# Conditioning and first norm: x loaded first, sums of squares, norm and splits in another order and in wider passes

## The chip, the cores and the metric

The kernel runs on one core of a Trainium2 chip. Its engines, as the profile names them: PE (TensorE, matrix products; PEld is its loading of the stationary operand), DVE (VectorE), ACT (ScalarE), POOL (GpSimd) and SP (SyncE, which here issues the DMAs). The metric is the device time of one execution in microseconds (us), as the median of several runs.

## The reference, cut to what matters

One layer of a hybrid diffusion backbone: 1024 latent tokens and 256 context tokens of width 1024. What the changed part computes is the conditioning, the first norm, the modulation and the operands of the input projection:

```python
sh1, sc1, ... = split(silu(c) @ w_ada + b_ada, 6)         # for the latents
cmods         = split(silu(c_ctx) @ w_ada + b_ada, 6)     # for the context
rmsnorm(x, g) = x * rsqrt(mean(x * x, axis=-1) + EPS) * g
h  = rmsnorm(x,   norm1_g) * (1 + sc1) + sh1
hc = rmsnorm(ctx, norm1_g) * (1 + cmods[1]) + cmods[0]
u  = h @ w_in                                             # 9280 columns
uc = hc @ w_in[:, :SSD_IN_WIDTH]
```

After it come a state-space scan, a Fourier branch, gates, an output projection and a feed-forward part; they are not touched.

## The kernel before

Activations lie transposed: channels on the 128 partitions, tokens along the free dimension. x is 8 tiles `xt[k]` of 128 x 1024, the context one tile `ct` of 128 x 8 x 256; k counts blocks of 128 channels. Products are taken in three passes: each operand is split into a rounded part (hi) and the rest (lo), and hi*hi + hi*lo + lo*hi is summed (`mm3m`, L210). So every normalised tile has to be cast (hi, on ACT) and subtracted (lo) before a product can use it, and so has every weight tile (`wsplit`, L198 and L199: hi on ACT, lo on GpSimd).

The first stage (L243 to L377) has these parts:

- *Conditioning.* `ada_k(hf, k)` (L259 to L265) multiplies the two vectors silu(c), silu(c_ctx) by one 512 KB weight tile `wa`: two matmuls of 2 x 512, which the profile shows as four records. hf = 0 gives shift and scale of the channel blocks 0 to 3, hf = 1 of 4 to 7. `ada_end(hf)` copies the result (`gr`, ACT), turns it onto partitions (`gtr`, 8 transposes) and makes `ada` and `sc1` of it on DVE. Five `wa` buffers are in turn.
- *Norm.* `sumsq` squares the 8 tiles on ACT and adds them on DVE; `rstd` sums the partitions with matmuls against a column of ones (`cps`, L287), adds EPS on DVE and takes the power -0.5 on GpSimd (L291); `rstd_bcast` makes diagonal blocks on DVE (L298) and spreads them over the partitions by a matmul (`bc`, L300, into PSUM).
- *Modulation.* For k < 4, x is multiplied by the broadcast (`normed`, L323, in halves of 512), scaled and shifted (L328), cast (L329), subtracted (L330). For k >= 4 the multiply takes the scale with it (L334), the cast the shift (L335). The context is multiplied by its broadcast (L352, eight instructions of 256), scaled and shifted on ACT (L338), cast on ACT (L339) and subtracted on GpSimd (L340), each per k.
- *First product.* `in_k` sums u's first 128 columns, for 512 + 512 latent and 256 context tokens, over k; what follows (the dt columns, the gate columns, pairs of blocks with sums of operands) runs on.

Inside this stage the order on PE and SP is the order in which the code is written (`manual_schedule`, L343). The order on DVE, ACT and GpSimd is laid out by a scheduler when the program is built; at run time it is fixed. Outside the stage the scheduler orders PE too, so products of the dt columns may lie between those of the first product. SP issues loads in the written order; `wraw` has two buffers, whi and wlo three.

In the written order before the change, the context's squares and column sums come first, x's after them, then x's broadcasts, `ada_k(1, 0)`, `ada_end(0)`, the modulation of k < 4, the other `ada_k(1, k)` and the first product.

Of the kernel before, what the change touches and what calls it, by code (L numbers as in the profile page):

```python
# [15 lines left out]
P = 128  # L16
D = 1024
KT = D // P
# [123 lines left out]
def _build(nc, tc, h, o, hook, stop, es):  # L142
# [86 lines left out]
    hc_hi = [hcpool.tile([P, LC], F32R, name=f"hchi{k}") for k in range(KT)]  # L229
    hc_lo = [hcpool.tile([P, LC], F32R, name=f"hclo{k}") for k in range(KT)]  # L230
# [13 lines left out]
    with pool("p0", "right") as p0, pool("pp0", "left", space=PSUM) as pp0:  # L244
# [22 lines left out]
        ada_load(0, 0)  # L267
        nc.sync.dma_start(out=ct, in_=h["cT"])
        ada_load(0, 1)
        for k in range(KT):  # L270
            nc.sync.dma_start(out=xt[k], in_=h["xT"][k])
            if k % 2 and k < 6:
                ada_load(0, 2 + k // 2)

        def sumsq(src, n, name):
            acc = p0.tile([P, n], F32, name=name)
            for k in range(KT):
                sq = acc if k == 0 else p0.tile([P, L], F32, name="sq", bufs=2)[:, :n]
                nc.scalar.activation(out=sq, in_=src(k), func=AF.Square)
                if k:  # L280
                    nc.vector.tensor_tensor(out=acc, in0=acc, in1=sq, op=ALU.add)
            return acc

        def rstd(sqacc, nt):
            cps = pp0.tile([P, 512], F32, name="cps", tag="cps", bufs=1)
            for t in range(nt):
                nc.tensor.matmul(cps[:, t:t + 1], lhsT=sqacc[:, t * P:(t + 1) * P], rhs=onec, start=True, stop=True)  # L287
# [37 lines left out]
        def modulated(k):  # L325
            sc, sh = sc1[:, 0, k:k + 1], ada[:, k, 0:1]
            if k < 4:
                nc.vector.tensor_scalar(out=xt[k], in0=xt[k], scalar1=sc, scalar2=sh, op0=ALU.mult, op1=ALU.add)  # L328
                nc.scalar.copy(out=h_hi[k], in_=xt[k])  # L329
                nc.vector.tensor_tensor(out=h_lo[k], in0=xt[k], in1=h_hi[k].bitcast(F32), op=ALU.subtract)  # L330
            else:
                for hf in range(2):
                    sl = slice(512 * hf, 512 * hf + 512)
                    nc.vector.scalar_tensor_tensor(out=xt[k][:, sl], in0=xt[k][:, sl], scalar=sc, in1=bcs[hf], op0=ALU.mult, op1=ALU.mult)  # L334
                nc.scalar.activation(out=h_hi[k], in_=xt[k], func=AF.Identity, bias=sh)  # L335
                nc.vector.scalar_tensor_tensor(out=h_lo[k], in0=xt[k], scalar=sh, in1=h_hi[k].bitcast(F32), op0=ALU.add, op1=ALU.subtract)
            cm = ct[:, k, :]
            nc.scalar.activation(out=cm, in_=cm, func=AF.Identity, scale=sc1[:, 1, k:k + 1], bias=ada[:, k, 1:2])  # L338
            nc.scalar.copy(out=hc_hi[k], in_=cm)  # L339
            nc.gpsimd.tensor_tensor(out=hc_lo[k], in0=cm, in1=hc_hi[k].bitcast(F32), op=ALU.subtract)  # L340

        gv = [[pp0.tile([P, 512], F32, name="gv", bufs=2) for _ in range(2)] for _ in range(2)]
        with tc.manual_schedule(engines={mybir.EngineType.PE, mybir.EngineType.SP}):  # L343
            ada_k(0, 0)
            csq = sumsq(lambda k: ct[:, k, :], LC, "csq")
            rsc = rstd(csq, 2)
            ada_k(0, 1)
            ada_k(0, 2)
            bcc = rstd_bcast(rsc, 0, 2)
            sqacc = sumsq(lambda k: xt[k], L, "sqacc")  # L350
            for k in range(KT):
                nc.vector.tensor_tensor(out=ct[:, k, :], in0=ct[:, k, :], in1=bcc[:, :LC], op=ALU.mult)  # L352
            for k in range(3, 6):
                ada_k(0, k)
            rs = rstd(sqacc, NT)
            for k in range(6, 8):
                ada_k(0, k)
            bcs = [rstd_bcast(rs, t0, 4) for t0 in (0, 4)]
            for k in range(4):
# [3 lines left out]
            ada_k(1, 1)  # L363
            for k in range(4):
                modulated(k)
            for k in range(2, 5):
                ada_k(1, k)
# [1333 lines left out]
```

## Time and profile before

| | |
|---|---|
| median of 3 runs | 2252.82 us (2246.53 to 2255.43) |
| profiled execution | 2255.23 us, span 2253.5 us |
| PE busy | 2164.4 us, 96% of the span |
| PEld busy | 1809.4 us, 80% |
| DVE busy | 1629.2 us, 72% |
| ACT busy | 991.6 us, 44% |
| POOL busy | 742.0 us, 33% |
| granted PE clock, mean | 0.987 |

The profile is of one execution. PE is busy nearly all the time; the busy share of its first fortieth of the span (56 us) is 7 tenths, as that of the last; of the others 8 or 9. A row of the timeline gives start, duration, engine, line, operation, output and inputs, how many instructions it merges, and in brackets how long the engine was idle ahead of it and what released it.

### The profile page before, as it was taken

Reading aid. Unit: us, or ns where it says so; the run is one execution under the profiler, and the core shown is the slowest. Engines: PE = TensorE matmul, PEld = TensorE weight load, DVE = VectorE, ACT = ScalarE, POOL = GpSimd, SP = SyncE. Lnnn points to the kernel's source line nnn. Section 1 sums busy time; section 2 is a strip of 40 time slices with the busy share of each in tenths; the row PEclk is TensorE's granted clock in tenths of the full one; section 3 lists DMA queues with packets and bytes.
Section 4 is the critical chain, followed back from the end, with each engine's and each line's share of the span. In section 5 each row is a group of like instructions: output and inputs, shape, how many; then the busy total and the mean of one; then the engine's idle time right before and its main releaser. Section 6 shows DMA issues by size and latency. Waiting matters only on the chain. (4 is left out here: it accounts for less than half of the span.)

```text
span 2253.5 us, 32731 instructions
## 1 busy us (share of the span) xinstructions
PE 2164.4 (96%) x11560; PEld 1809.4 (80%) x11560; DVE 1629.2 (72%) x2783; ACT 991.6 (44%) x2082; POOL 742.0 (33%) x610
## 2 busy tenths in 40 slices
PE   7999999999999999999999999998898999999997
PEld 1778888877889999999889887786676888887876
DVE  5888888997757777777636558826987567675578
ACT  4445444545345676676733212124422332334443
POOL 1532211010236455555521132144333333332222
PEclk8999999999999999999999999999899999999999
DMA  7222223333455455555454547541476234457765
GB/s 281 76 71 84 85 85 122 133 130 108 144 165 172 157 164 179 165 169 175 151 202 161 183 152 264 188 159 63 155 270 229 85 114 155 152 190 240 234 203 181
DMA packets 167101, 360.28 MB, mean 160 GB/s; under 512 B 17548, under 2 KB 57228, under 8 KB 166296
## 3 DMA queue, kind: packets, MB, share of 16 engines
q1 hardware_dynamic: 166936, 358.18, 47.7%
q8 instruction: 91, 1.49, 0.3%
q14 instruction: 74, 0.61, 0.1%
HBM read 267.34 MB, written 90.78 MB: 159 GB/s over the span
## 5 line engine op out<-in xcount | busy, mean ns | idle before, releaser
L199 POOL TENSOR_TENSOR wlo<-wraw,whi 128x1024 fp32r<-128x1024 f32 (+1 forms) x83 | 203.0, 2449 | 614.4 <-ACT whi L198 566.8
L203 PE MATMUL fill<-whi,hhi 128*128 128x256 f32 x768 | 222.4, 291 | 0.0
L198 ACT CAST whi<-wraw 128x1024 fp32r<-128x1024 f32 (+1 forms) x123 | 126.5, 1034 | 215.7 <-PE dm L210 82.9
L433 DVE SCALAR_TENSOR_TENSOR cv<-pad,vecs,cv 128x1282 f32<-128x1282 f32 (+1 forms) x128 | 211.0, 1678 | 9.1 <-ACT cv L430 8.7
L204 PE MATMUL fill<-wlo,hhi 128*128 128x256 f32 x768 | 215.8, 281 | 0.6 <-POOL wlo L199 0.6
L205 PE MATMUL fill<-whi,hlo 128*128 128x256 f32 x768 | 216.0, 282 | 0.0
L915 ACT ACTIVATE abc<-abc,a_all 128x128 f32<-128x128 f32 x512 | 157.8, 390 | 96.2 <-DMA abc<-s_a 93.4
L203 PE MATMUL fp<-m,oph 128*128 128x512 f32 x452 | 180.3, 400 | 12.5 <-ACT oph L1384 10.5
L205 PE MATMUL fp<-m,opl 128*128 128x512 f32 x452 | 180.4, 400 | 9.6 <-DVE opl L1385 6.7
L204 PE MATMUL fp<-m,oph 128*128 128x512 f32 x452 | 180.2, 399 | 0.0
L496 PE MATMUL mm<-tq,whi 128*128 128x512 f32 x480 | 153.9, 401 | 2.3 <-ACT whi L198 2.3
L203 PEld LDWEIGHTS fill<-whi,hhi 128*128 128x128 f32 x768 | 144.1, 188 | 2.2 <-ACT ust L807 0.4
L204 PEld LDWEIGHTS fill<-wlo,hhi 128*128 128x128 f32 x768 | 144.6, 188 | 1.6 <-POOL wlo L199 0.8
L205 PEld LDWEIGHTS fill<-whi,hlo 128*128 128x128 f32 x768 | 144.3, 188 | 0.5
L496 PE MATMUL mm<-hhi,whi 128*128 128x512 f32 x320 | 128.2, 402 | 3.4 <-DVE pad L572 3.4
L496 PE MATMUL mm<-hlo,whi 128*128 128x512 f32 x320 | 127.6, 399 | 0.0
L496 PE MATMUL mm<-hhi,wlo 128*128 128x512 f32 x320 | 127.6, 400 | 0.0
L203 PEld LDWEIGHTS fp<-m,oph 128*128 128x128 f32 x452 | 85.9, 190 | 34.2 <-ACT oph L1384 11.7
L205 PEld LDWEIGHTS fp<-m,opl 128*128 128x128 f32 x452 | 85.6, 189 | 33.8 <-DVE opl L1385 9.7
L917 DVE COPY_PREDICATED abc<-misc,abc 128x512 f32<-128x512 int32 x64 | 50.8, 793 | 85.0 <-ACT abc L915 84.8
L496 PEld LDWEIGHTS mm<-tq,whi 128*128 128x128 f32 x480 | 89.7, 189 | 23.7 <-ACT whi L198 3.4
L891 DVE SCALAR_TENSOR_TENSOR S<-S,ead,st 128x64 f32<-128x64 f32 x512 | 104.7, 271 | 0.0
(411 smaller groups left out, 5929.4 us busy)
## 6 DMA issues: line engine op xcount, KB each, us to landing
abc<-s_a SPq DMA_DIRECT2D x64, 512.0 KB
fraw<-in_wfi SPq DMA_DIRECT2D x44, 512.0 KB
wraw<-in_wxbc SPq DMA_DIRECT2D x32, 512.0 KB
dx<-in_wada SPq DMA_DIRECT2D x32, 512.0 KB
wraw<-in_wzf SPq DMA_DIRECT2D x24, 512.0 KB
gt<-s_gate SPq DMA_DIRECT2D x24, 512.0 KB
fi<-in_wfo SPq DMA_DIRECT2D x22, 512.0 KB
s_cw<-fo SPq DMA_DIRECT2D x44, 256.0 KB
```

The costliest lines, as they stand in the source:

```text
L198: nc.scalar.copy(out=hi[:, :cols], in_=raw[:, :cols])
L199: (eng or nc.gpsimd).tensor_tensor(out=lo[:, :cols], in0=raw[:, :cols], in1=hi[:, :cols].bitcast(F32), op=ALU.subtract)
L203: nc.tensor.matmul(ps, lhsT=a[0], rhs=b[0], start=start, stop=False)
L204: nc.tensor.matmul(ps, lhsT=a[0], rhs=b[1], start=False, stop=False)
L205: nc.tensor.matmul(ps, lhsT=a[1], rhs=b[0], start=False, stop=stop)
L433: nc.vector.scalar_tensor_tensor(out=v[:, :n], in0=pd[:, t:t + n], scalar=cwh[:, 5 * b + t:5 * b + t + 1], in1=v[:, :n], op0=ALU.mult, op1 ...
L496: nc.tensor.matmul(ps, lhsT=lhs[x], rhs=b[i][y], start=i == 0 and (x, y) == (0, 0), stop=i == 3 and (x, y) == (1, 0))
L891: nc.vector.scalar_tensor_tensor(out=sn[:, hd_], in0=S[-1][:, hd_], scalar=decp[:, i, d, 4 * g + j:4 * g + j + 1], in1=sv_[:, hd_], op0=AL ...
L915: nc.scalar.activation(out=abc[:, d, j, :], in_=abc[:, d, j, :], func=AF.Identity, scale=-1.0, bias=a_all[:, c, hd:hd + 1])
L917: nc.vector.copy_predicated(out=E, mask=tri_b.bitcast(mybir.dt.int32)[:, None, :].to_broadcast([P, HPG, P]), data=abc[:, 1])
```

## The change

All of it lies in the first stage.

- SP loads x and the first four `wa` tiles in turn, then the fifth `wa`, the context, the first projection weights, the dt weights and the next five `wa`. The loads of the gate weights and of two later projection tiles stand ahead of the last of the `wa`.
- x's squares, column sums and broadcasts come before the context's. The context is squared in two passes of 1024 and added in one (`ctx_squares`); its column sums take four matmuls per 128 tokens, where one was enough. They stand behind x's broadcasts on PE, its broadcast behind `ada_k(1, 1)`.
- The context's multiply is one instruction of 2048.
- Modulation is the same for all k: `normed` for all eight, then cast with scale and shift on ACT (L338), scale and shift in place on DVE (L339), subtraction on DVE (L340). The context's cast and subtraction take four k at once, the subtraction on DVE (L348). The first weight tile's lo is taken on DVE.
- `in_k` of k = 0 to 3 stands before `ada_end(1)`, where only k = 0 did.

```diff
--- before.py
+++ after.py
@@ -226,8 +226,8 @@
     nc.sync.dma_start(out=rows, in_=h["rows"].broadcast_to([P, 160]))
     phA = ExitStack()
     hcpool = phA.enter_context(pool("hcpool", "right"))
-    hc_hi = [hcpool.tile([P, LC], F32R, name=f"hchi{k}") for k in range(KT)]
-    hc_lo = [hcpool.tile([P, LC], F32R, name=f"hclo{k}") for k in range(KT)]
+    hch2, hcl2 = [[hcpool.tile([P, 4, LC], F32R, name=f"{nm}{hf}") for hf in range(2)] for nm in ("hchi", "hclo")]
+    hc_hi, hc_lo = [[t[k // 4][:, k % 4, :] for k in range(KT)] for t in (hch2, hcl2)]
 
     ppm = phA.enter_context(pool("ppm", "left", space=PSUM))
 
@@ -264,27 +264,38 @@
             for s in range(2):
                 nc.tensor.matmul(gv[hf][s][:2, :], lhsT=sv[:, :, k], rhs=w[:, s, :], start=(k == 0), stop=(k == KT - 1))
 
-        ada_load(0, 0)
-        nc.sync.dma_start(out=ct, in_=h["cT"])
-        ada_load(0, 1)
         for k in range(KT):
             nc.sync.dma_start(out=xt[k], in_=h["xT"][k])
-            if k % 2 and k < 6:
-                ada_load(0, 2 + k // 2)
-
-        def sumsq(src, n, name):
-            acc = p0.tile([P, n], F32, name=name)
+            if k % 2 == 0:
+                ada_load(0, k // 2)
+        ada_load(0, 4)
+        nc.sync.dma_start(out=ct, in_=h["cT"])
+
+        def sq_tile():
+            return p0.tile([P, L], F32, name="sq", bufs=2)
+
+        def x_squares():
+            acc = p0.tile([P, L], F32, name="sqacc")
             for k in range(KT):
-                sq = acc if k == 0 else p0.tile([P, L], F32, name="sq", bufs=2)[:, :n]
-                nc.scalar.activation(out=sq, in_=src(k), func=AF.Square)
+                sq = sq_tile() if k else acc
+                nc.scalar.activation(out=sq, in_=xt[k], func=AF.Square)
                 if k:
                     nc.vector.tensor_tensor(out=acc, in0=acc, in1=sq, op=ALU.add)
-            return acc
-
-        def rstd(sqacc, nt):
+            return lambda t: [acc[:, t * P:t * P + P]]
+
+        def ctx_squares():
+            c = [sq_tile() for _ in range(2)]
+            for hf in range(2):
+                nc.scalar.activation(out=c[hf], in_=ct[:, 4 * hf:4 * hf + 4, :].rearrange("p a b -> p (a b)"), func=AF.Square)
+            nc.vector.tensor_tensor(out=c[0], in0=c[0], in1=c[1], op=ALU.add)
+            return lambda t: [c[0][:, q * LC + t * P:q * LC + t * P + P] for q in range(4)]
+
+        def rstd(parts, nt):
             cps = pp0.tile([P, 512], F32, name="cps", tag="cps", bufs=1)
             for t in range(nt):
-                nc.tensor.matmul(cps[:, t:t + 1], lhsT=sqacc[:, t * P:(t + 1) * P], rhs=onec, start=True, stop=True)
+                ps = parts(t)
+                for q, a_ in enumerate(ps):
+                    nc.tensor.matmul(cps[:, t:t + 1], lhsT=a_, rhs=onec, start=q == 0, stop=q == len(ps) - 1)
             ms = p0.tile([P, 16], F32, name="ms", bufs=2)
             nc.vector.tensor_scalar(out=ms[:, :nt], in0=cps[:, :nt], scalar1=EPS, scalar2=None, op0=ALU.add)
             rs = p0.tile([P, 16], F32, name="rs", bufs=2)
@@ -324,56 +335,54 @@
 
         def modulated(k):
             sc, sh = sc1[:, 0, k:k + 1], ada[:, k, 0:1]
-            if k < 4:
-                nc.vector.tensor_scalar(out=xt[k], in0=xt[k], scalar1=sc, scalar2=sh, op0=ALU.mult, op1=ALU.add)
-                nc.scalar.copy(out=h_hi[k], in_=xt[k])
-                nc.vector.tensor_tensor(out=h_lo[k], in0=xt[k], in1=h_hi[k].bitcast(F32), op=ALU.subtract)
-            else:
-                for hf in range(2):
-                    sl = slice(512 * hf, 512 * hf + 512)
-                    nc.vector.scalar_tensor_tensor(out=xt[k][:, sl], in0=xt[k][:, sl], scalar=sc, in1=bcs[hf], op0=ALU.mult, op1=ALU.mult)
-                nc.scalar.activation(out=h_hi[k], in_=xt[k], func=AF.Identity, bias=sh)
-                nc.vector.scalar_tensor_tensor(out=h_lo[k], in0=xt[k], scalar=sh, in1=h_hi[k].bitcast(F32), op0=ALU.add, op1=ALU.subtract)
-            cm = ct[:, k, :]
-            nc.scalar.activation(out=cm, in_=cm, func=AF.Identity, scale=sc1[:, 1, k:k + 1], bias=ada[:, k, 1:2])
-            nc.scalar.copy(out=hc_hi[k], in_=cm)
-            nc.gpsimd.tensor_tensor(out=hc_lo[k], in0=cm, in1=hc_hi[k].bitcast(F32), op=ALU.subtract)
+            nc.scalar.activation(out=h_hi[k], in_=xt[k], func=AF.Identity, scale=sc, bias=sh)
+            nc.vector.tensor_scalar(out=xt[k], in0=xt[k], scalar1=sc, scalar2=sh, op0=ALU.mult, op1=ALU.add)
+            nc.vector.tensor_tensor(out=h_lo[k], in0=xt[k], in1=h_hi[k].bitcast(F32), op=ALU.subtract)
+
+        def ctx_modulated(hf):
+            for k in range(4 * hf, 4 * hf + 4):
+                cm = ct[:, k, :]
+                nc.scalar.activation(out=cm, in_=cm, func=AF.Identity, scale=sc1[:, 1, k:k + 1], bias=ada[:, k, 1:2])
+            cm = ct[:, 4 * hf:4 * hf + 4, :]
+            nc.scalar.copy(out=hch2[hf], in_=cm)
+            nc.vector.tensor_tensor(out=hcl2[hf], in0=cm, in1=hch2[hf].bitcast(F32), op=ALU.subtract)
 
         gv = [[pp0.tile([P, 512], F32, name="gv", bufs=2) for _ in range(2)] for _ in range(2)]
         with tc.manual_schedule(engines={mybir.EngineType.PE, mybir.EngineType.SP}):
-            ada_k(0, 0)
-            csq = sumsq(lambda k: ct[:, k, :], LC, "csq")
-            rsc = rstd(csq, 2)
-            ada_k(0, 1)
-            ada_k(0, 2)
-            bcc = rstd_bcast(rsc, 0, 2)
-            sqacc = sumsq(lambda k: xt[k], L, "sqacc")
-            for k in range(KT):
-                nc.vector.tensor_tensor(out=ct[:, k, :], in0=ct[:, k, :], in1=bcc[:, :LC], op=ALU.mult)
-            for k in range(3, 6):
+            raw0 = wp.tile([P, 1024], F32, name="wraw", bufs=NRAW)
+            nc.sync.dma_start(out=raw0, in_=h["wxbc"][0])
+            for k in range(5):
                 ada_k(0, k)
-            rs = rstd(sqacc, NT)
-            for k in range(6, 8):
+            rs = rstd(x_squares(), NT)
+            for k in range(5, 8):
                 ada_k(0, k)
             bcs = [rstd_bcast(rs, t0, 4) for t0 in (0, 4)]
+            rsc = rstd(ctx_squares(), 2)
             for k in range(4):
                 normed(k)
             ada_k(1, 0)
             ada_end(0)
             ada_k(1, 1)
+            bcc = rstd_bcast(rsc, 0, 2)
+            nc.vector.tensor_tensor(out=ct, in0=ct, in1=bcc[:, None, :LC].to_broadcast([P, KT, LC]), op=ALU.mult)
+            w0 = wsplit(raw0, eng=nc.vector)
             for k in range(4):
                 modulated(k)
-            for k in range(2, 5):
-                ada_k(1, k)
-            w0 = wload(h["wxbc"][0])
-            for k in range(5, 8):
+                if k == 0:
+                    ctx_modulated(0)
+            for k in range(4, KT):
+                normed(k)
+            for k in range(2, 8):
                 ada_k(1, k)
             pss0 = [in_ps() for _ in range(3)]
-            in_k(pss0, w0, 0, True)
+            for k in range(4):
+                in_k(pss0, w0, k, True)
             ada_end(1)
             for k in range(4, KT):
                 modulated(k)
-            for k in range(1, KT):
+                if k == 4:
+                    ctx_modulated(1)
+            for k in range(4, KT):
                 in_k(pss0, w0, k, True)
     if hook is not None:
         hook("h_hi", h_hi)
```

On PE, from x's column sums to the first product, before the change (cps are column sums, gv the conditioning, bc x's broadcasts, gtr the transposes, the last row the first product):

```order
L287 MATMUL cps<-onec,sqacc 128x1 x8
L265 MATMUL gv<-wa,sv 2x512 x4
L300 MATMUL bc<-sq,misc 128x512 x2
L265 MATMUL gv<-wa,sv 2x512 x2
L310 MATMUL gtr<-misc,gr 128x2 x8
L265 MATMUL gv<-wa,sv 2x512 x14
L210 MATMUL mm<-hhi_190,whi 128x512 x2
```

The same stretch of PE after the change (cps from sq are the context's column sums, mm from sq its broadcast):

```order
L298 MATMUL cps<-onec,sqacc 128x1 x8
L265 MATMUL gv<-wa,sv 2x512 x6
L311 MATMUL bc<-sq,misc 128x512 x2
L298 MATMUL cps<-onec,sq 128x1 x8
L265 MATMUL gv<-wa,sv 2x512 x2
L321 MATMUL gtr<-misc,gr 128x2 x8
L265 MATMUL gv<-wa,sv 2x512 x2
L311 MATMUL mm<-sq,misc 128x256
L265 MATMUL gv<-wa,sv 2x512 x12
L210 MATMUL mm<-hhi_190,whi 128x512 x2
```

The context's column sums and broadcast, which stood ahead of this stretch, now stand in it, the sums behind bc and ahead of all gv of the second half.

On DVE, from x's column sums to the scales, before the change (xt are the tiles of x, numbers are buffers, bc PSUM):

```order
L289 TENSOR_SCALAR ms<-cps 128x8
L298 TENSOR_SCALAR sq<-misc,rs 128x128 x8
L323 TENSOR_TENSOR xt_248<-xt_248,bc 128x512
L323 TENSOR_TENSOR xt_249<-xt_249,bc 128x512
L323 TENSOR_TENSOR xt_250<-xt_250,bc 128x512
L323 TENSOR_TENSOR xt_251<-xt_251,bc 128x512
L323 TENSOR_TENSOR xt_248<-xt_248,bc 128x512
L323 TENSOR_TENSOR xt_249<-xt_249,bc 128x512
L323 TENSOR_TENSOR xt_250<-xt_250,bc 128x512
L323 TENSOR_TENSOR xt_251<-xt_251,bc 128x512
L313 TENSOR_TENSOR ada<-gtr,vecs 128x8 x2
L316 SCALAR_TENSOR_TENSOR sc_180<-ada,vecs 128x2x4
```

The end of the same stretch of DVE after the change; eight more L334, of the first half of the tokens, stand ahead of its first row:

```order
L334 TENSOR_TENSOR xt_236<-xt_236,bc 128x512
L334 TENSOR_TENSOR xt_237<-xt_237,bc 128x512
L334 TENSOR_TENSOR xt_238<-xt_238,bc 128x512
L334 TENSOR_TENSOR xt_239<-xt_239,bc 128x512
L334 TENSOR_TENSOR xt_240<-xt_240,bc 128x512
L334 TENSOR_TENSOR xt_241<-xt_241,bc 128x512
L334 TENSOR_TENSOR xt_242<-xt_242,bc 128x512
L334 TENSOR_TENSOR xt_243<-xt_243,bc 128x512
L290 TENSOR_TENSOR sq<-sq 128x1024
L300 TENSOR_SCALAR ms<-cps 128x2
L309 TENSOR_SCALAR sq<-misc,rs 128x128 x2
L324 TENSOR_TENSOR ada<-gtr,vecs 128x8 x2
```

Sixteen multiplies stand where eight did, and the addition of the context's squares (L290), which stood far ahead as L281, stands behind them.

## Rows read from the trace of the kernel before

**Rows 1.** Timeline of PE, 0 to 60 us: start, duration, what, count, idle before.

```profile
7.77 3.19 PE L265 MATMUL gv<-wa,sv 128*2 128x512 f32 x4 [7.77 <-DMA wa<-in_wada]
...
16.08 5.86 PE L265 MATMUL gv<-wa,sv 128*2 128x512 f32 x8
21.87 0.70 PE L300 MATMUL mm<-sq,misc 128*128 128x256 f32 x2
22.50 3.60 PE L265 MATMUL gv<-wa,sv 128*2 128x512 f32 x8
26.80 1.88 PE L265 MATMUL gv<-wa,sv 128*2 128x512 f32 x4 [0.70 <-DMA wa<-in_wada]
31.94 3.54 PE L287 MATMUL cps<-onec,sqacc 128*128 128x1 f32 x16 [3.26 <-DVE sqacc L281]
35.41 6.43 PE L265 MATMUL gv<-wa,sv 128*2 128x512 f32 x8
41.77 1.98 PE L300 MATMUL bc<-sq,misc 128*128 128x512 f32 x4
43.69 1.88 PE L265 MATMUL gv<-wa,sv 128*2 128x512 f32 x4
45.50 0.66 PE L310 MATMUL gtr<-misc,gr 2*128 2x2 f32 x8
46.09 12.18 PE L265 MATMUL gv<-wa,sv 128*2 128x512 f32 x28
58.20 0.73 PE L210 MATMUL mm<-hhi,whi 128*128 128x512 f32 x2
```

**Rows 2.** Timeline of PE, 60 to 140 us: its waits.

```profile
66.96 0.74 PE L210 MATMUL mm<-hhi,whi 128*128 128x512 f32 x2 [0.74 <-ACT hhi L335]
...
68.58 0.44 PE L210 MATMUL mm<-hhi,whi 128*64 128x512 f32 x1 [0.53 <-DVE xt L334]
...
133.57 0.79 PE L496 MATMUL mm<-tq,wlo 128*128 128x512 f32 x1 [3.32 <-DVE wlo L199]
```

**Rows 3.** Windows of PE: stretch, length, PE busy (count), granted clock, DMA share, GB/s.

```profile
30.00:32.00 2.00, 0.06 (x1) 0.73 0.99 377
...
40.00:42.00 2.00, 2.00 (x4) 0.71 0.81 252
```

**Rows 4.** Timeline of ACT, 0 to 75 us: squares of the context and of x.

```profile
10.15 0.42 ACT L279 ACTIVATE csq<-ct 128x256 f32<-128x256 f32 x1 [3.85 <-DMA ct<-in_cT]
...
21.17 1.06 ACT L279 ACTIVATE sq<-xt 128x1024 f32<-128x1024 f32 x1 [1.29 <-DVE sqacc L281]
...
29.17 1.06 ACT L279 ACTIVATE sq<-xt 128x1024 f32<-128x1024 f32 x1 [0.27 <-DVE sqacc L281]
```

**Rows 5.** Timeline of DVE, 0 to 60 us.

```profile
22.61 2.73 DVE L352 TENSOR_TENSOR ct<-ct,mm 128x256 f32<-128x256 f32 x8 [1.47 <-PE mm L300]
25.26 6.53 DVE L281 TENSOR_TENSOR sqacc<-sqacc,sq 128x1024 f32<-128x1024 f32 x5
...
37.45 1.66 DVE L298 TENSOR_SCALAR sq<-misc,rs 128x128 f32<-128x128 f32 x8 [1.76 <-POOL rs L291]
42.94 4.87 DVE L323 TENSOR_TENSOR xt<-xt,bc 128x512 f32<-128x512 f32 x8 [3.83 <-PE bc L300]
```

**Rows 6.** Timelines of DVE, ACT and POOL, 70 to 160 us.

```profile
75.44 0.68 DVE L471 TENSOR_TENSOR sm<-hhi,hlo 128x512 f32<-128x512 f32 x1
...
103.19 1.77 DVE L534 TENSOR_TENSOR wraw<-wraw 128x512 f32<-128x512 f32 x1 [5.19 <-POOL wlo L199]
...
132.31 1.21 DVE L199 TENSOR_TENSOR wlo<-wraw,whi 128x1024 fp32r<-128x1024 f32 x1
...
99.63 1.05 ACT L198 CAST whi<-wraw 128x1024 fp32r<-128x1024 f32 x1 [0.33 <-PE mm L210]
...
100.76 2.40 POOL L199 TENSOR_TENSOR wlo<-wraw,whi 128x1024 fp32r<-128x1024 f32 x1 [8.88 <-ACT whi L198]
```

**Rows 7.** Waits of PE, 70 to 700 us: total, times, longest.

```profile
PE mm L496 <- DVE pad L572: 3.4, 1, 3.4
```

## The prediction

> **What bounds the kernel now.** I read the page first: PE is busy for 96% of the span, so only time in which PE stands still, or runs at its lower clock, can be won or lost. Slice 1 of 40 is the poorest one, and the whole change lies in it and the next. So I read PE's timeline from 0 to 60 us [rows 1]. The reader should see three things there. PE sums the modulation vectors (gv) from 7.77 us on, four records per weight tile. It stands still until DVE has added the latent squares, at 31.94. From there to 58.20, the first projection product, it never waits again: column sums, two gv tiles (8 records, 35.41 to 41.84), the two broadcasts, one tile, eight transposes, seven tiles. In this stage PE, not DVE or ACT, ends last. From the end of the sixteenth gv matmul (41.84, below: E) to the first product are 16.35 us.
>
> The clock is the second view [rows 3]: granted 0.73 in 30 to 32 and 0.71 in 40 to 42, that is 2.4 GHz until about 30.9, 1.2 GHz until about 41.2. One gv record takes 0.435 us at 2.4 GHz (12.18 / 28, [rows 1]), so about 0.85 at 1.2.
>
> The third view is PE after 60 us [rows 2]: waits of 0.74 and 0.53 us for the second half of the latent tiles, and 3.32 us at 130.25 for a weight split on DVE.
>
> **The change part by part.** *Loads.* Between the context's landing (10.15 us, ACT's wait) and the sixth gv tile's (26.80, PE's wait) lie 13 loads of 512 KB [rows 1, 4]: 1.28 us each. The first load lands at 7.77. The new order puts the last latent tile 12th, so at 7.77 + 11 x 1.28 = 21.9 us; gv tiles six to eight are numbers 17.5 to 19.5 and land at 28.9, 30.2 and 31.5. Before, the last square of x began at 29.17, and the column sums 2.74 us later [rows 1, 4]. In the old kernel x's additions stood behind eight context multiplies: the square begun at 21.17 was ready at 22.23, its addition ran at 25.26 [rows 4, 5]. Now nothing precedes them, and PE can sum at 21.9 + 2.74 = 24.6 instead of 31.94.
>
> *From there to E.* PE has gv tiles one to five beside the loads (9 to 24.8 us at 2.4 GHz, to 27.4 if all at 1.2), then the column sums: 3.47 us at 1.2 GHz [rows 1], for which the trace shows no duration at 2.4 GHz; half of it, 1.74, is the other bound. They end between 26.6 and 30.9. Then three gv tiles, 12 records. In the trace the 8 records after column sums take 5.79 us (16.08 to 21.87) and 6.36 (35.41 to 41.77): 5 to 7 of them at 1.2 GHz. So I take 6 and 6: 5.1 + 2.6 = 7.7 us, from 28.9 (the load) or 30.9: E = 36.6 to 38.6. I take 37.5. Bounds: 33.2 (the eighth tile lands at 31.5 and all is at 2.4 GHz) and 41.2 (all at 1.2). Won: 41.84 - 37.5 = 4.3 us. The diagonals (3.7 us from the end of the sums to the end of the eight, [rows 1, 5]) and the split of the first weight tile, now on DVE (1.21 us, [rows 6]), end by 36 us and are hidden by the gv tiles.
>
> *From E to the first product.* Here PE's hand-written order gets a wait that it did not have. Behind the two broadcasts now stand the context's column sums. They need DVE's addition of the two context squares, and in DVE's queue that addition stands behind all 16 multiplies of x by the broadcast (before: 8, and nothing of PE waited for them). Behind the sums on PE stand all 8 gv tiles of the second half, and so every product. Step by step, from E:
> - broadcast to the first multiply: 1.1 us (41.84 to 42.94)
> - 16 multiplies at 4.87 / 8 = 0.61: 9.74 us [rows 5]
> - addition 1.22 (as the additions of x), handover 0.12: 1.34 us
> - context column sums, again 16 records: 3.47 us at 1.2 GHz, since PE has stood still for some 10 us
> - gv tile nine, 4 records at 0.85: 3.41; transposes 0.68 (45.41 to 46.09); tile ten, 2 records at each clock: 2.57; the context's broadcast, moved here, 0.63 (21.87 to 22.50)
> - six tiles, 24 records at 0.435: 10.44 us.
>
> Sum 33.4 us, against 16.35: 17.0 us lost. The context squares on ACT, wide as one of x (2 x 1.06 us, [rows 4]), wait for the second broadcast (E + 2.0, to free their buffers) and for the cast of the gate weights, whose load is issued when GpSimd has split the dt weights behind the power of x, near 35 us. They are ready by 42 to 43; the addition runs at E + 10.8 = 48.3, so they are not last. If the multiplies were slowed by GpSimd's two splits beside them, this would be up to 2.4 us more (the split of 100.76 us, [rows 6]).
>
> Does DVE do what stands behind other work only in its turn? The rows show it: 3 us between ready (22.23) and run (25.26), behind eight multiplies [rows 4, 5]. [...]
>
> *Other edits.* Wider squares, the wide context multiply, the fused scale on ACT and the context splits on DVE all lie between the transposes and the first product, beside some 14 us of gv on PE. DVE has there 4 scalings (at most 1.2 us each, as a 1024-wide addition), one wide multiply (between 1.2 and 2.7 us, a 1024-wide addition and the eight narrow multiplies that it replaces, [rows 5]; I take 2.2, near the eight, since the elements are as many), and 4 + 1 subtractions of 1.21: 13 us, and 1.06 before it for ACT's first cast. That just fits and I cost it at nothing; without the cover it is 1 us. The second half of the latent tiles is now normalised beforehand, and 52 products of the dt projection stand before the first that needs the context's second half: the waits of 0.74 and 0.53 [rows 2] go, 1.3 us.
>
> *Sum.* +17.0 - 4.3 - 1.3 = +11.4 us. The 3.32 us wait at 130 stays: DVE's work ahead of it starts at 103.19 after a wait for GpSimd's split (100.76), that for ACT's cast (99.63), that for PE to release the buffer [rows 6]. It moves with PE. The profiled execution took 2255.23 us (span 2253.5), 2.4 above the median of the runs, 2252.82; I put the difference on the median: 2264.
>
> **The rivals.**
> - *The clock stays up.* If short pauses leave PE at 2.4 GHz, E = 33.2, and the second sum loses 1.7 (column sums) and 2.5 (six records): 29.2 us. First product at 62.4, +4.2 - 1.3 = +2.9: 2256. For: loads come every 1.28 us and PE is hardly idle before 27. Against: at 30.9 the clock fell 2.2 us after gv work [rows 3].
> - *Not slower: the later waits pay it back.* PE arrives 11 us later at places where it waited for DVE: 3.32 us at 130, 3.4 us for DVE L572 further on [rows 7]. If DVE is not tied to PE there, it is ahead, and both go, 6.7 us: 2257. It decides if DVE's weight combinations still start near 103 us. Against: the chain 99.63, 100.76, 103.19 hangs on PE.
> - *Slower still: DVE falls behind.* Four k tiles with the transposes take 8.0 us of PE (58.20 to 66.22, [rows 1, 2]), so the second half's scales come near 70.9 + 8.0 + 0.6 = 79.5 us, and with ACT's cast, 4 scalings and 5 subtractions DVE is through near 91, where it was 75.44 [rows 6]: 16 us later, PE only 11. If the gaps of DVE up to 103.19 don't take up these 4 to 5 us, the wait at 130 grows by them: 2268. An E of 41.2 gives the same.
> - *The change doesn't do what it says*: DVE adds the context squares ahead of most multiplies. The squares are there at E + 2.0 + 2.1 = 41.6 us, so the addition runs 6.7 us earlier than 48.3: +4.7, 2257.5. Against: the order of DVE's queue.
>
> **How the numbers follow.** The sum's own case 0.62, spread 2259 to 2269 by the bounds of E and of the pauses; slower still 0.15; clock stays up 0.08; paid back 0.08; the last rival 0.02; the rest, something that I don't see, 0.05. About 0.5% (11.3 us) is what a measurement of this kernel can tell from no change, and the sum lies just on it: its chance divides in halves, 0.31 slower and 0.31 same. Same: 0.31 + 0.08 + 0.08 + 0.02 = 0.49. Slower: 0.31 + 0.15 = 0.46. Faster: 0.05. The range, of 8 in 10, reaches from the first rival to the third: 2256 to 2269.
>
> **What would show it.** In the new trace: column sums of x at about 24 to 27 us; a pause of PE of about 10 us that ends with the context's column sums, put down to DVE L290, with 16 rows of DVE L334 back to back in it; granted clock 0.5 after it; the first product near 70 us, and no waits in its second half; DVE's weight combinations near 114. Wrong if PE's pause is under 5 us, if the first product comes before 62, or if PE's later waits shrink by more than 3 us.

## The result, and the profile after

The change makes the kernel slower by 0.8%: 2272.66 us median of 5 runs (2265.76 to 2277.69), against 2254.72 for the kernel before beside them; ratio 1.0083, 95% interval 1.0054 to 1.0111. The forecast was 2264, range 2256 to 2269; the measured median lies 3.7 us above the range. The profiled execution took 2265.76 us (span 2263.4), the fastest of its five; it stands 10.5 us above the profiled execution of before.

PE's timeline of the changed kernel answers to [rows 1] and [rows 2] (start, duration, what, count, idle before):

```profile
25.28 1.95 PE L298 MATMUL cps<-onec,sqacc 128*128 128x1 f32 x16
29.19 5.31 PE L265 MATMUL gv<-wa,sv 128*2 128x512 f32 x12 [1.97 <-DMA wa<-in_wada]
34.44 1.98 PE L311 MATMUL bc<-sq,misc 128*128 128x512 f32 x4
46.54 3.55 PE L298 MATMUL cps<-onec,sq 128*128 128x1 f32 x16 [10.12 <-DVE sq L290]
50.01 3.57 PE L265 MATMUL gv<-wa,sv 128*2 128x512 f32 x4
53.52 1.01 PE L321 MATMUL gtr<-misc,gr 2*128 2x2 f32 x8
54.46 3.58 PE L265 MATMUL gv<-wa,sv 128*2 128x512 f32 x4
57.96 0.73 PE L311 MATMUL mm<-sq,misc 128*128 128x256 f32 x2
58.62 10.46 PE L265 MATMUL gv<-wa,sv 128*2 128x512 f32 x24
...
69.01 0.73 PE L210 MATMUL mm<-hhi,whi 128*128 128x512 f32 x2
...
143.04 0.51 PE L505 MATMUL mm<-tq,wlo 128*128 128x512 f32 x1 [3.31 <-DVE wlo L199]
```

The column sums of x come 6.7 us earlier than in [rows 1] (25.28 for 31.94), and E, the end of the sixteenth gv matmul, at 34.50 for 41.84. Then the new pause: 10.12 us until DVE has added the context squares. Everything behind it is late by what the pause and the lower clock behind it (granted 0.50 from 44 to 58 us) cost, and the first product comes 10.8 us later than before. The waits of 0.74 and 0.53 us of [rows 2] are gone (a new one of 0.42 us, for the scales, stands at 77.25); the one of 3.3 us is there unchanged, 9.5 us later.

DVE in the same execution (answers to [rows 5] and [rows 6]), and then ACT's context squares, say what the pause waits for:

```profile
35.60 9.66 DVE L334 TENSOR_TENSOR xt<-xt,bc 128x512 f32<-128x512 f32 x16 [2.61 <-PE bc L311]
45.17 1.22 DVE L290 TENSOR_TENSOR sq<-sq 128x1024 f32<-128x1024 f32 x1
...
89.71 0.68 DVE L480 TENSOR_TENSOR sm<-hhi,hlo 128x512 f32<-128x512 f32 x1
...
112.71 0.69 DVE L543 TENSOR_TENSOR wraw<-wraw 128x512 f32<-128x512 f32 x1 [2.57 <-POOL wlo L199]
```

```profile
37.47 2.00 ACT L289 ACTIVATE sq<-ct 128x1024 f32<-128x1024 f32 x2
```

Sixteen multiplies back to back, then the addition. ScalarE had its inputs ready at 39.47 (squares begun at 37.47, 2.00 us), and it ran at 45.17, 5.70 us later, when the multiplies ahead of it in the queue were done.

The granted clock by windows (stretch, length, busy time of each engine with its count, clock, DMA share, GB/s), for [rows 3]:

```profile
30.00:40.00 10.00, 6.42 (x15) 1.44 (x13) 7.39 (x17) 3.90 (x5) 2.77 (x2) 1.00 0.99 379
40.00:50.00 10.00, 3.46 (x16) 3.49 (x16) 6.39 (x10) 0.00 (x0) 0.00 (x0) 0.55 0.16 59
50.00:60.00 10.00, 10.00 (x23) 2.28 (x23) 3.10 (x8) 4.63 (x4) 0.71 (x1) 0.60 0.28 69
60.00:70.00 10.00, 10.00 (x27) 2.47 (x25) 8.86 (x9) 4.27 (x7) 0.00 (x0) 1.00 0.83 300
```

PE enters the pause at a granted clock of 1.00 (30 to 40 us) and leaves it at 0.50 (in every window of 2 us from 44 to 58): the same 16 column-sum records take 1.95 us at 25.28 and 3.55 at 46.54, and four gv records 1.88 at 23.47 and 3.57 at 50.01. Where the prediction and the expectations give the clock as a frequency, no profile shows one: the traces of before and of the changed kernel record granted shares, and only 1.00 and 0.50. "The lower clock" below is the granted 0.50.

### The profile page after: what moved, and what is told of

Its sections match the earlier page's. It is cut to its first block, busy times and chain, and to the rows that moved or that the text cites. A ratio compares the mean times of both kernels' runs of the same rounds, so it can differ in the third digit from the quotient of the medians.

```text
span 2263.4 us, 32725 instructions
## 1 busy us (share of the span) xinstructions
PE 2164.9 (96%) x11572; PEld 1811.2 (80%) x11572; DVE 1625.6 (72%) x2777; ACT 991.7 (44%) x2070; POOL 727.2 (32%) x601
## 4 chain that ended last, share of the span: by engine, by line
PE 68%; DVE 13%; DMA 8%; ACT 4%; issue 4%; POOL 2%; SPq 0%; POOLq 0%; DVEq 0%; ACTq 0%
PE mm L505 15%; PE dm L210 8%; PE fp L205 5%; PE fp L204 5%; PE fp L203 5%; DMA abc<-s_a 4%; ACT abc L924 3%; PE fill L210 2%; PE mm L507 2%; PE spq L210 2%; PE fq L204 2%; PE fq L205 2%; PE fq L203 2%; PE mm L210 2%; PE fill L203 2%
## 5 line engine op out<-in xcount | busy, mean ns | idle before, releaser
L203 PEld LDWEIGHTS fp<-m,oph 128*128 128x128 f32 x452 | 85.9, 190 | 33.2 <-ACT oph L1393 11.6
```

Source lines behind the costliest of these rows:

```text
L203: nc.tensor.matmul(ps, lhsT=a[0], rhs=b[0], start=start, stop=False)
```

## The experiments

All but the last four were run for two questions: is the pause the loss, and what lies behind the first stage? "Transposes" below is the start of the first input transposes, behind the whole first stage. It is 122.21, 121.39 and 121.99 us in three profiles of the kernel before (mean 121.9).

| kernel | median us (runs) | ratio, 95% interval | first product | transposes |
|---|---|---|---|---|
| before, beside the experiments | 2254.84 (79) | | 58.2, 57.4, 57.8 | 121.9 |
| e1 changed kernel again | 2267.82 (6) | 1.0068, 1.0053 to 1.0084 | 71.3 | 133.9 |
| e2 late context sums | 2263.55 (6) | 1.0051, 1.0035 to 1.0066 | 56.5 | 126.7 |
| e3 addition on GpSimd | 2265.81 (6) | 1.0060, 1.0043 to 1.0077 | 64.3 | 126.9 |
| e4 filled pause | 2266.67 (6) | 1.0054, 1.0039 to 1.0069 | 68.5 | 131.1 |
| e5 fused norm for 4 to 7 | 2269.51 (6) | 1.0066, 1.0042 to 1.0090 | 64.4 | 133.4 |
| e6 all repairs, fused | 2261.35 (12) | 1.0030, 1.0015 to 1.0044 | 54.5 | 122.7 |
| e7 late sums, x first | 2256.44 (12) | 1.0006, 0.9990 to 1.0022 | 58.1 | 123.1 |
| e8 norm alone on before | 2264.81 (12) | 1.0049, 1.0034 to 1.0064 | 56.7 | 128.8 |
| e9, e11 changed kernel again | 2272.09 (4), 2266.88 (4) | 1.0081, 1.0060 | 71.8, 69.9 | 134.5, 132.5 |

**e1: the changed kernel unchanged.**

> The changed kernel once more, for its spread: its profiled execution was 10.5 us longer than that of before (2265.76 against 2255.23), its median 18 us. Theory A, the wait and the clock behind it are all: a second profile shows again a PE wait of about 10 us ahead of the context's column sums, the first product near 69 us, and the ratio to before lies near 1.005. Theory B, a second loss lies elsewhere and the profiled execution happened to miss it: ratio near 1.008, and the new profile is 5 to 8 us longer than the first, with the difference behind the first stage.

The pause is there again (10.12 us), the first product 2.25 us later than in the first profile. The ratio, 1.0068, lies between the 1.005 of theory A and the 1.008 of B. The profiled execution took 2274.48, and 6.5 of its 8.7 us over the first profile lie behind the first stage: the second question, taken up with e9 to e12.

**e2: the context's sums where PE has other work.**

```
-            rsc = rstd(ctx_squares(), 2)      # behind the two broadcasts
 ...
+            for k in range(2, 6):
+                ada_k(1, k)
+            rsc = rstd(ctx_squares(), 2)
+            ada_k(1, 6)
             bcc = rstd_bcast(rsc, 0, 2)
```

> The context's column sums stand behind six gv tiles of the second half on PE, its broadcast behind the seventh, all else as in the changed kernel. Theory A: PE goes on from x's broadcasts at about 36.4 us, the six tiles end near 47.6, where the addition on DVE (46.4) is done; no wait of 10 us, clock at 2.4 GHz; the products are then held by the context's cast and split, so the first stage's products are in flow about 9 us earlier than in the changed kernel: ratio to before 0.998 to 1.003. Theory B (the loss is not that wait): ratio stays at 1.007 to 1.009.

PE's timeline:

```profile
54.07 0.70 PE L311 MATMUL mm<-sq,misc 128*128 128x256 f32 x2 [0.85 <-DVE sq L309]
...
62.10 0.58 PE L210 MATMUL mm<-hchi,whi 128*128 128x256 f32 x1 [4.86 <-ACT hchi L347]
```

The pause shrinks from 10.12 to 0.85 us, and the gv tiles end at 56.5 instead of 69.0. But half comes back as a new wait: the third product needs the context's cast, which is now what is late. Transposes at 126.7 where the changed kernel has 131.7 to 134.5. The ratio, 1.0051, is outside both forecasts: theory A had named this hold but still expected 9 us of gain, where 6.5 are left at the transposes; theory B had none.

**e3: the addition on GpSimd**, so that it doesn't stand behind the multiplies (`nc.vector` to `nc.gpsimd` in the context's addition).

> One instruction moved: the addition of the two context squares runs on GpSimd, so it no longer stands behind the 16 multiplies on DVE. Theory A: squares ready at 39.5 us, addition 2.4 us on GpSimd, column sums at about 42 instead of 46.5, first product near 64.5 instead of 69: 4 to 5 us less than the changed kernel, ratio to it about 0.998. If the order on DVE does not matter (the squares themselves are late, or the broadcast ends last): column sums still at 46 to 47, no gain.

```profile
42.36 2.88 PE L298 MATMUL cps<-onec,sq 128*128 128x1 f32 x16 [3.89 <-POOL sq L290]
...
64.26 0.73 PE L210 MATMUL mm<-hhi,whi 128*128 128x512 f32 x2
...
1310.84 0.47 PE L210 MATMUL dm<-dx,whi 128*128 128x512 f32 x1 [2.11 <-DVE gt L1279]
```

The pause falls to 3.89 us with nothing else changed in the stage: it was VectorE's queue, not the squares, that PE waited for. The stage comes 6.3 us earlier (mean 133.2 to 126.9); the median follows it by only 2 us against e1 beside it and by 4.4 against all 19 runs of the changed kernel.

The last row shows where a good part of the rest went. In e2, e3, e4 and e8 the scheduler has laid out PE's products between 1280 and 1390 us in another order than in the kernel before, the changed kernel, e5, e6 and e7. PE waits there for VectorE (2.11 us here; 1.08, 1.97 and 2.37 us in e2, e4 and e8), and the others have no such wait. Against the kernel before, these four come out of that place, in one profile each, 2.2 (e2), 3.2 (e3 and e4) and 5.1 us (e8) later than they went in. So much of their medians is not the first stage's.

**e4: the pause filled** with products of constants into an unused tile, so that PE stays busy.

```
+            fl = in_ps()
+            for i in range(11):
+                nc.tensor.matmul(fl, lhsT=ones, rhs=misc[:, 0:4, :], start=i == 0, stop=i == 10)
             rsc = rstd(ctx_squares(), 2)
```

> Eleven products of constants, whose result nobody uses, stand on PE between x's broadcasts and the context's column sums; they are as long as the wait. Theory A: the wait stays (column sums at 46.5) but the clock stays at 2.4 GHz, so sums 1.95 instead of 3.55, the two gv tiles 1.9 instead of 3.6 each, transposes 0.66 instead of 1.01: first product at 63.5 instead of 69, 5 to 6 us less than the changed kernel. If the pause alone costs and the clock does not: within 1 us of the changed kernel.

PE's timeline, and then its windows:

```profile
37.94 9.61 PE L362 MATMUL mm<-misc 128*128 128x512 f32 x22
48.22 1.92 PE L298 MATMUL cps<-onec,sq 128*128 128x1 f32 x16 [0.68 <-DVE sq L290]
...
53.95 3.58 PE L265 MATMUL gv<-wa,sv 128*2 128x512 f32 x4
```

```profile
40.00:48.00 8.00, 7.54 (x18) 3.05 (x16) 8.00 (x13) 0.00 (x0) 0.00 (x0) 1.00 0.22 82
48.00:52.00 4.00, 3.78 (x19) 2.16 (x20) 0.71 (x4) 0.00 (x0) 0.70 (x1) 0.83 0.02 4
52.00:58.00 6.00, 6.00 (x16) 1.57 (x14) 2.60 (x6) 3.54 (x4) 0.00 (x0) 0.54 0.38 131
```

The clock stays up through the filled pause (granted 1.00 from 36 to 48 us) and the column sums take 1.92 us instead of 3.55, but it falls behind them (0.83 from 48 to 52, 0.54 from 52 to 58), though PE had been idle for only 0.68 us. So the stretch at the lower clock is only moved: about 2 us won at the first product, where theory A had 5 to 6 and its rival at most 1. The pause itself is the larger part.

**e5: features 4 to 7 normed as before**, fused in their own modulation, so that 8 multiplies stand ahead of the addition (core of the diff):

```
-            for k in range(4, KT):
-                normed(k)
 ...
+                    nc.vector.scalar_tensor_tensor(out=xt[k][:, sl], in0=xt[k][:, sl], scalar=sc, in1=bcs[hf], op0=ALU.mult, op1=ALU.mult)
```

> The changed kernel, but features 4 to 7 are normed in one fused pass by their own modulation, as the kernel before does it, so that only 8 instead of 16 multiplications of x stand on VectorE ahead of the addition of the context squares. All that follows the first stage then stands in the order of the kernel before, instruction for instruction; with the changed kernel's norm the scheduler places some transposes, weight splits and convolution steps otherwise up to about 230 us. Theory A (the wait of 10 us is the loss ahead of 130 us, and the rest of the loss comes from the other order behind it): the wait shrinks by 8 x 0.60 = 4.8 us to 5.3, the first product comes at about 64.5, the wlo wait at about 138 instead of 143, and the median falls to about 2258 (2253.3 + 4.7). Rival B (the later loss comes with any shift of the first stage, whatever the order): the same first stage, but a median of 2264 to 2266, as the run with the addition on GpSimd had it.

```profile
43.99 3.55 PE L298 MATMUL cps<-onec,sq 128*128 128x1 f32 x16 [5.33 <-DVE sq L290]
...
75.86 1.22 PE L210 MATMUL mm<-hhi,whi 128*128 128x512 f32 x2 [3.61 <-ACT hhi L346]
...
78.10 0.69 PE L210 MATMUL mm<-hhi,whi 128*64 128x512 f32 x1 [0.30 <-DVE xt L345]
```

The pause shrinks as forecast to 5.33 us and the first product comes at 64.4. Then feature 4, whose norm now waits for the last modulation, is 3.61 us late, and PE runs it more slowly (0.69 us for a record that took 0.44 before, [rows 2]; granted 0.87 from 60 to 80 us, where before has 1.00). At the transposes nothing of the gain is left, 133.4, so both theories' times missed. The order behind the stage is that of before here, and yet the median lies 14.7 us above before, 3 more than the 11.6 that the stage has lost: theory A, by which the later order makes that rest, finds no support.

**e6: all repairs at once, with the fused norm** (e5, sums behind the third and broadcast behind the sixth tile, and e7's order of products).

> The changed kernel with all repairs at once: features 4 to 7 fused as before; column sums of the context squares behind the third and broadcast behind the sixth gv tile of the second half, so that PE does not stand for them; in the first weight block the x products of features 0 to 3 ahead of their context products. The order behind the first stage is that of the kernel before. Theory A: no wait above 1.5 us between 40 and 65 us, first product at about 55.7 (58.2 before), the clock at full level from 40 to 60 us, the wlo wait 2.5 to 3.5 us earlier than the kernel before has it (134 there), and a median of about 2250, 0.15% faster than before. Rival B: the first stage as for A, but a median of 2254 to 2257, since a later loss of 4 to 6 us remains.

PE's timeline and a window of it:

```profile
64.57 0.86 PE L210 MATMUL mm<-hhi,whi 128*128 128x512 f32 x2 [1.97 <-ACT hhi L352]
...
66.81 0.69 PE L210 MATMUL mm<-hhi,whi 128*64 128x512 f32 x1 [0.29 <-DVE xt L351]
```

```profile
60.00:70.00 10.00, 7.65 (x35) 4.80 (x34) 8.97 (x14) 7.18 (x9) 1.90 (x1) 0.75 0.00 0
```

The first product comes 3.7 us earlier than in [rows 1], and the wait for feature 4 (1.97 us) with the fallen clock (granted 0.75 from 60 to 70 us) takes that back: 122.7. Both theories had expected a lead of 2.5 to 3.5 us there. With the later order of before, the median still is 6.5 us above before. Of that the stage has made 0.9; what makes the rest stays open.

**e7: the change's own norm, late sums, x products first** in the first weight block (e2, and):

```
             for k in range(4):
-                in_k(pss0, w0, k, True)
+                in_part(pss0, w0, k, True)     # x columns
             ada_end(1)
 ...
+            for k in range(4):
+                in_part(pss0, w0, k, False)    # context columns
```

> The changed kernel with its own norm in two passes (and so with its own order behind the first stage), but with the late context sums of the second experiment and the x products of features 0 to 3 ahead of their context products. It has nearly the first stage of the run with all repairs, with the later order of the changed kernel. Theory A: the 4.9 us hold for hchi goes, the wlo wait comes at about 132 (134 before), and the median is 2255 to 2258, 4 to 6 us above what the first stage alone would give. Rival B: the same first stage and the same median as the run with all repairs, within 2 us.

```profile
55.67 0.70 PE L317 MATMUL mm<-sq,misc 128*128 128x256 f32 x2 [0.86 <-DVE sq L315]
...
58.10 0.73 PE L210 MATMUL mm<-hhi,whi 128*128 128x512 f32 x2
```

From 36 us to the transposes PE waits for nothing longer than 2.1 us. The transposes come at 123.1, and the time is that of the kernel before. That lies within A's numbers, but A had it 4 to 6 us above what the first stage gives; rival B had it level with e6, and it is 5 below. PE's order behind its stage is the changed kernel's but for some places up to 161 us and from 520 to 560, and it loses nothing there (1.6 us in the median, 1.3 of them in the stage). So A falls, with e5 and e6: the changed kernel's later order is not the loss. This is the best version of the change, 0.6% below the changed kernel's 2270.2 of 19 runs and not faster than before.

**e8: the norm alone, on the kernel before** (L327 to L336 of before replaced by the change's three lines, features 4 to 7 normed with the others).

> The kernel before with one part of the change alone: the norm of x in its own pass for all eight features, and the modulation as one activation on ScalarE with a multiply-add and a subtraction on VectorE; loads, context and sums stay as before, and the order behind the first stage is nearly that of before. Theory A: VectorE gets 8 x 0.6 us of multiplications more and loses the dearer fused forms, so the combos start at 75 to 80 us as before or a little later; the wait of 0.74 for hhi goes; a median within 2 us of 2253. Rival (VectorE's added passes are themselves the later loss): 2256 to 2258.

PE's timeline, then ACT's and POOL's:

```profile
59.75 0.39 PE L210 MATMUL mm<-hchi,whi 128*128 128x256 f32 x1 [2.35 <-ACT hchi L332]
...
63.88 0.58 PE L210 MATMUL mm<-hclo,whi 128*128 128x256 f32 x1 [3.28 <-POOL hclo L333]
```

```profile
59.30 0.71 ACT L332 CAST hchi<-ct 128x256 fp32r<-128x256 f32 x2
```

```profile
62.12 3.76 POOL L333 TENSOR_TENSOR hclo<-ct,hchi 128x256 fp32r<-128x256 f32 x4
```

Both numbers missed: the median is 10 us above before. The sixteen multiplies (9.66 us for the 4.87 of eight, [rows 5]) hold up the scales, ScalarE casts the context at 59.30, GpSimd splits it at 62.12 behind a weight split, and PE waits 5.6 us; the products behind it run at a lower granted clock (0.74 from 60 to 80 us, 1.00 in before; eight transposes take 1.01 us for 0.66 in [rows 1]). The stage has lost 6.9 us at the transposes; the place near 1300 us (see e3) adds 5.1. So this part doesn't pay alone; with the context's splits on VectorE and the context last (e7) it does no harm.

**e9 to e12: the changed kernel twice and the kernel before twice**, for their profiles.

> The changed kernel once more, for another profile. In the first two profiles of it the spans at the lower clock behind the first 100 us, the last wait at the output not counted, came to 34.1 us (time 2265.76) and 54.6 us (2274.48), against 34.1 us in the one profile of before (2255.23). Theory C (the loss beyond the first stage is the clock: waits of 1 to 3.5 us that both kernels have let it fall in some executions and not in others, and half of such a span is lost; the first stage costs 9 to 12 us in every run): the first product comes at 69 to 72 us as in the other two, and the time follows the spans, about 2266 where they come to 34 us and half of whatever they are longer. Rival D (a wait of the changed kernel behind the first stage is longer in every run): PE falls behind before at the same place in all profiles, with the same spans at the lower clock.

> The kernel before, unchanged, for a second profile. Theory C: the place and number of the spans at the lower clock differ from those of the first profile although every instruction is the same, between 24 and 48 us behind the first 100 us; the first product at 58 to 59 us. Rival D: the same spans as in the first profile, 34.1 us, at the same places, within 3.4 us.

> The changed kernel, a fourth profile. Theory C: as for the third, spans at the lower clock of 30 to 60 us behind the first stage at changing places, the time following half of them. Rival D: the loss behind the first stage at the same places as in the third profile.

> The kernel before, a third profile. Theory C: spans at the lower clock of 24 to 48 us behind the first stage, at other places than in the first two profiles; where the three profiles of before have clearly less in the mean than the four of the changed kernel (by 10 us or more), the changed kernel's waits fall unluckily more often, and the difference is worth half of that. Rival D: the same spans as in the first two.

e10 and e12 (before) had medians of 2254.10 and 2255.05. Summed over windows of 20 us from 100 to 2240 us, the time at the lower clock (40 us times what the granted clock of a window lacks of 1.00) is 34.8, 44.8 and 38.4 us in the three profiles of before and 34.8, 56.0, 42.4 and 34.8 in the four of the changed kernel: means of 39.3 and 42.0. The spells differ between executions of one kernel, as C has it, and D falls as an account of the whole; but the difference of the means, 2.7 us, is under the 10 set for "unlucky more often". The clock of all runs says the same: its mean is 0.9850 in 19 runs of the changed kernel and 0.9877 in 79 of before, which makes some 12 us more at the lower clock, and 11 of them lie between 20 and 100 us (below). One place shows how chance enters. The same wait for the scan's state S, in the first profile of the changed kernel and in e1, each with the windows behind it (PE alone):

```profile
850.66 0.67 PE L890 MATMUL st<-xwf,bh 128*128 128x256 f32 x2 [1.92 <-DVE S L900]
```

```profile
851.00:853.00 2.00, 2.00 (x17) 1.00 0.38 106
853.00:855.00 2.00, 2.00 (x17) 1.00 0.52 144
```

```profile
855.55 0.75 PE L890 MATMUL st<-xwf,bh 128*128 128x256 f32 x2 [1.88 <-DVE S L900]
```

```profile
855.00:857.00 2.00, 1.45 (x5) 0.75 0.65 190
857.00:859.00 2.00, 2.00 (x12) 0.50 0.20 66
859.00:861.00 2.00, 2.00 (x15) 0.89 0.65 198
```

After 1.92 us of waiting the granted clock stays at 1.00, after 1.88 us it falls for some 3.4 us (0.75, 0.50 and 0.89 in the three windows). It falls in e9 too (2.56 us of waiting; 0.92 from 840 to 860 us) and not in e11 (1.95; 1.00). In before this wait is 1.37, 0.12 and 1.77 us and the clock stays up (1.00 from 840 to 860 us in all three profiles), so at this one place the changed kernel does wait longer in every profile, as D has it. Between 20 and 100 us the time at the lower clock is 17.2, 20.8, 27.2 and 17.2 us in the changed kernel, against 10.8, 8.8 and 9.2 before: this is the change's, in every profile.

## Why the prediction was right in its mechanism and wrong in its time

- **Loads and E.** Forecast: sums of x at 24.6, E at 37.5. Measured sums at 25.28; the broadcasts behind E begin at 34.4, 36.3, 36.7 and 35.4 in four profiles (before 41.8, 41.0, 41.3): won 5.7 us in the mean instead of 4.3. The 12 records are the main reason: forecast 7.7 us, measured 5.31 in the first profile and in e11, 7.01 in e1, and 8.04 in e9, by the clock (granted 1.00, 1.00, 0.91 and 0.83 from 20 to 40 us):

```profile
28.73 8.04 PE L265 MATMUL gv<-wa,sv 128*2 128x512 f32 x12 [1.97 <-DMA wa<-in_wada]
36.69 1.98 PE L311 MATMUL bc<-sq,misc 128*128 128x512 f32 x4
```

- **From E to the first product.** Forecast 33.4 us against 16.35; measured 34.6, 35.0, 35.1 and 34.5 against 16.4. In the first profile, from the start of x's broadcasts: 1.16 to the first multiply (forecast 1.1, from the end of the gv tiles), 9.57 multiplies (9.74), 1.37 addition and handover (1.34), 3.47 column sums (3.47), 3.51 tile nine (3.41), 0.94 transposes (0.68), 3.50 tile ten (2.57), 0.66 broadcast (0.63), 10.39 for 24 records (10.44). Only the clock's return was placed too early, within tile ten instead of behind it (granted 0.50 from 56 to 58 us, 0.99 from 58 to 60). (The forecast's 0.68 for the transposes counts from 45.41, which no row has; [rows 1] has them at 45.50, so 0.59.) Lost 18.4 instead of 17.0; with E the two errors cancel, which is luck, and the first product comes 12.7 us late in the mean, the 17.0 - 4.3 of the forecast. GpSimd's split beside the multiplies (2.37 us from 36.69) cost them nothing (0.60 us each, 0.61 in [rows 5]).
- **The other waits.** PE is 1.4 us less late at the transposes than at the first product, in all four profiles (forecast 1.3). Transposes 11.3 us late in the mean (133.2 against 121.9), where the sum was 11.4. The wait at 130 stayed at 3.3 us, VectorE's sums of operands start at 89.7 (forecast near 91) and its weight combinations at 112.7 (forecast near 114): "slower still" and "paid back" are both refuted, and so is "doesn't do what it says". "The clock stays up" came true ahead of E in two of four profiles (12 records in 5.31 us), but behind E, where it would have saved 4.2 us, in none (granted 0.57, 0.59, 0.53 and 0.57 from 40 to 60 us).
- **The step that failed** is the last one, "I put the difference on the median: 2264", with its range up to 2269. It took the 11.4 us of the first stage for the whole cost, put what lies behind 130 us at nothing, stood on a median of three runs, and its range had no term for the spread of executions. The runs show in its place:
  - *The cost* is 15.4 us in the mean of all runs (2269.9 in 19 of the changed kernel against 2254.5 in 79 of before, 2 us either way), not 11.4. The first stage made 11.3 of them, as summed. Another 0.5 lies outside the profiled span, in every run: the time is 2.29 us above the span in the mean of the 19 and 1.79 in that of the 79. Then 1.3 is what the profiles show behind the stage (mean span 2266.95 us in four of the changed kernel and 2254.33 in three of before, 12.6 apart). The last 2.2 us the profiles don't show: the three profiled executions of before are 1.6 us slower than its mean, the four of the changed kernel 0.6 faster than theirs.
  - *The base* was 2254.8, the median of the 79, not the 2252.8 of three runs.
  - *The spread.* The sets of 4 to 6 runs of the changed kernel have medians of 2272.66, 2267.82, 2272.09 and 2266.88, and all 19 runs have 2270.2 (2263.3 to 2277.7). The set on record lies 2.4 us above its own kernel's median. That it fell outside the range was in part its luck: two of the other three sets lie within.

  Whether the 3.5 us that are neither the stage's nor outside the span are made behind the stage in every run stays open; profiles whose spans spread by 11 us in the changed kernel can't tell. It is not the clock's doing for the most part (1 to 3 us more at the lower clock behind 100 us, about half of that in time, since a gv record takes 0.435 us at 1.00 and 0.89 at 0.50). Against a loss in every run speaks e7, 0.3 us more than its stage's 1.3. For it speak e5 and e6, 3.1 and 5.6 us more than their stages'. e3 doesn't: 3.2 of the 6 us that it has over its stage come from the place near 1300 us, which the changed kernel lacks.

## What to carry to other kernels

Here a reduction put into PE's order behind another engine's queue cost its whole wait (10.12 us), and the lower clock after it (3.55 us for 1.95 of column sums); moved behind matmuls whose inputs were already there, it cost its own 2 us (1.95 in e7), but then the next operand down the line had to be looked at too (e2 to e7). Parts of the change were not additive: a fused pass that shortened one queue made the operand behind it late (by 3.61 us in e5, 1.97 in e6), and a part that is harmless in its set (e7) loses 7 us in the first stage alone (e8). An edit in one place can also move the scheduler's order a thousand us behind it, here for 2 to 5 us (e2, e3, e4, e8): a median then doesn't measure the edit alone. A forecast from one profiled execution needs the spread between executions as a term of its own, here up to 11 us between profiles of one kernel.

## What the runs showed of the hardware that was not expected

- Pauses of 0.7 to 2.0 us between gv tiles, from 15 to 29 us, with 1.88 us of work between them, left the granted clock at 1.00 in the first profile of the changed kernel (15 to 31 us) and in e11 (20 to 40 us; 12 records in 5.31 us in both). In e1 and e9 it fell: 0.91 and 0.83 from 20 to 40 us, and the 12 records took 7.01 and 8.04 us.
- A wait of 1.9 us let the clock fall in one execution (1.88 us in e1, granted 0.50 from 857 to 859 us) and not in another of the same kernel (1.92 us in the first profile, 1.00 from 849 to 863).
- After 9.61 us of filled pause at a granted clock of 1.00 the clock fell: 0.83 from 48 to 52 us, 0.54 from 52 to 58. PE had been idle for 0.68 us and had run 16 column sums of one column each (1.92 us). Where the 0.83 is a fall that lasts to the end of its window, it came near 50.6 us, in gv tile nine, some 3 us behind the filler: an estimate from these windows (e4).
- One multiply of 128x2048 took 2.29 us where eight of 128x256 took 2.73 [rows 5].
